# A recurrent two-layer step: one head's turn on TensorE, whole-row transposes through DRAM, and eight matmuls of ones

## The chip, the cores and the metric

The kernel runs on one core of a Trainium2 chip. Its time is the device time of one execution in microseconds. Before the change it takes 2245.49 us, the median of three runs (2245.31 to 2247.33). A core has five engines with one instruction queue each, all served in order: TensorE (PE, with its weight loads as PEld), VectorE (DVE), ScalarE (ACT), GpSimd (POOL) and SyncE (SP), which only issues DMAs here.

## What is computed

One inference step of a two-layer decoder with D = 1024, run for a prompt of 1024 tokens and for 8 samples of one token each, with the same weights. Cut to what matters:

```
for layer in (even, odd):
    shift, scale, gate = split(silu(c) @ ada_w[layer] + ada_b[layer])
    h = rms(x) * (1 + scale) + shift
    even: gated delta rule, 8 heads of 128x128; mLSTM, 8 heads of 64x128
        h_b = sigmoid(o_pre) * rms(mlstm(q_b, k_b, v_b, i, f))
    odd:  gated linear attention (GLA), 4 heads of 128x256; retention, 4 heads of 128x256
    y = concat(branch outputs) * silu(z)        # 2048 wide
    x = x + gate * (y @ w_out)
y = rms(x), and the new states of every head, for prompt and samples
```

All of it is float32, chunk by chunk over the prompt.

## The kernel before

Prompt and samples stand side by side as W = 1032 columns, features on the 128 partitions (feature layout). A matmul of float32 accuracy is three matmuls of values split into a high and a low part (hi x hi, hi x lo, lo x hi) over three pieces of NB = 344 columns. The high part is a rounding copy on ScalarE (`whi`, or an activation tile such as `s_h`), the low part a subtraction on VectorE or POOL (`wlo`). Weights come in blocks of 128 columns (`wf` loaded, `whi`, `wlo`). PSUM banks are named `pj` (three, projections), `A` (three) and `B` (two). SBUF tiles are named slots that are used over and over: `s_zz`, `s_mp`, `s_va` and so on.

Nothing is issued where it is written. A class `Recorder` collects every operation with its operands, and its `order` (line 274) plans the whole program as a list schedule, ten times forward and backward, by a table of costs (`_cost`, line 106, and `_pe_cost`, line 136), and keeps the order with the shortest plan. `emit` (line 443) then issues it, so that every row of the profile has line 448, and rows are told apart by tiles. An edit anywhere can change the order on all engines.

At the start, the ada matmuls of the even layer run group by group (g = 0 to 3), each from four 512-KB loads of `in_ada_w` that lie in free slots. They give the scale and shift of two feature tiles (through bank B, `s_qg` and `base`), and with these VectorE makes h in pieces of 344 columns (`s_aT`, `s_Y` and others in, `s_h` out). The first weight block is projected into the A banks as the h tiles come.

In the even layer each gated-delta head h makes `s_q` (line by line: a causal convolution of four taps in `s_pt`, then SiLU), normalizes it, and multiplies keys with queries (A<-s_q,s_k). The gates of all heads are scanned once; their values go from row layout to token layout through DRAM (`ed` written from `s_Y`, read as `s_N`).

An mLSTM head ends with its output in token layout, `hn`, in slot `mp`. `mlstm_out` (line 1525) turns it to feature layout: `squares` (line 1697) transposes 32x32 squares of a whole 128x1024 tile in one VectorE instruction, writes it to DRAM (`td`) in four DMAs and reads it back in one; four VectorE products with the norm weight and the output gate (`zz`) follow. Heads 0 to 6 write the product to DRAM (`yd`); head 7 keeps it for the output projection, as its 16th block (k = 15).

`out_proj` (line 1943) splits the 16 blocks of y into high and low parts, each in one piece of 1032 columns (`split`), where k = 14 and 15 are used last (`late`). They multiply weights kept in `s_zz` (even) or `s_tmp` (odd).

In the odd layer a GLA or retention head needs its keys in token layout (`kt`, slot `N`). `by_token` (line 1690) makes them by 16 VectorE transposes of 32x256, one for each pair of 32-row squares; values go through `squares` (`v_tokens`, line 1710), followed by a copy on ScalarE. Retention scales its keys on ScalarE after that.

## Time and profile before

| | |
|---|---|
| runs | 2247.33, 2245.31, 2245.49 us |
| profiled execution | 2242.51 us, of which 2240.7 us span |
| mean granted TensorE clock | 0.989 |
| TensorE busy | 2174.0 us (97%), 17532 matmuls |
| VectorE busy | 1307.6 us (58%) |
| ScalarE, POOL busy | 762.3 us (34%), 586.7 us (26%) |
| DMA | 290.62 MB, 130 GB/s on average |

Times are microseconds from the start of the span. A row of the timeline has start, duration, engine, line, operation, output tile, input tiles, shape and count, and in brackets the idle time of the engine ahead of it with what ended that. Busy times of TensorE overlap between neighbours (an instruction's end is modelled), so the distance between starts is what one costs. The layout of time by the loads of weights: those of the even layer's output projection are issued from 1078.8 to 1276.0 us, those of the odd layer's input projection from 1287.3 to 1962.5, and those of its output projection from 1974.4 to 2183.1.

### The profile page before, as it was taken

How to read it: one execution, taken by the hardware profiler on the slowest of the kernel's cores; microseconds unless marked ns; L12 is line 12 of the kernel's file. 1: busy time of each engine (PE TensorE's matmuls, PEld its weight loads, DVE VectorE, ACT ScalarE, POOL GpSimd, SP SyncE). 2: the span in 40 equal slices, each digit the busy share in tenths (PEclk: the TensorE clock that was granted, in tenths of full speed). 3: DMA queues.
4: the chain of work that ended last, by engine and by line, in shares of the span. 5: the costliest groups of instructions: out<-in, count | busy, mean ns of one | idle time of the engine just before them, and what ended most of it. 6: DMA issues, size and time to landing. Idle time of an engine off the chain costs nothing.

```text
span 2240.7 us, 42464 instructions
## 1 busy us (share of the span) xinstructions
PE 2174.0 (97%) x17532; PEld 2027.2 (90%) x17532; DVE 1307.6 (58%) x2559; ACT 762.3 (34%) x1374; POOL 586.7 (26%) x409
## 2 busy tenths in 40 slices
PE   6989999999999999999989999999999999999998
PEld 4877788898999899899989999999999999999997
DVE  6766747575665758576553265745754754756322
ACT  4422323232423333232331134235234334334322
POOL 3121222111221212211330042523523522534110
PEclk9999999999999999998999999999999999999999
DMA  9466564436352544346483223344253253365212
GB/s 265 125 205 149 168 174 145 120 90 175 89 152 66 171 124 121 108 120 155 134 237 109 65 77 85 88 144 124 68 168 111 77 162 117 96 183 197 69 59 93
DMA packets 343352, 290.62 MB, mean 130 GB/s; under 512 B 51963, under 2 KB 315637, under 8 KB 343150
## 3 DMA queue, kind: packets, MB, share of 16 engines
q1 hardware_dynamic: 343158, 287.91, 44.6%
q8 instruction: 137, 2.24, 0.4%
q14 instruction: 57, 0.47, 0.1%
HBM read 213.61 MB, written 74.44 MB: 129 GB/s over the span
## 4 chain that ended last, share of the span: by engine, by line
PE 80%; DVE 8%; DMA 7%; issue 2%; POOL 1%; ACT 1%; SPq 1%; POOLq 0%; DVEq 0%; ACTq 0%
PE pj L448 63%; PE A L448 12%; PE B L448 4%; DMA s_tmp<-sd 1%; SPq L448 1%; DVE arena L448 1%; DVE s_pt L448 1%; DVE s_tmp L448 1%; DMA s_tmp<-in_state_gla 1%; DVE s_N L448 1%; POOL s_qg L448 1%; DVE s_zz L448 1%; DVE wlo L448 1%; DVE s_h L448 1%; DMA s_Y<-rd 1%
## 5 line engine op out<-in xcount | busy, mean ns | idle before, releaser
L448 PE MATMUL pj<-s_h,whi 128*128 128x344 f32 (+1 forms) x6024 | 1487.4, 326 | 3.5 <-ACT whi L448 1.3
L448 PEld LDWEIGHTS pj<-s_h,whi 128*128 128x128 f32 (+1 forms) x6024 | 1038.7, 188 | 33.2 <-issue 20.8
L448 PE MATMUL pj<-s_h,wlo 128*128 128x344 f32 (+1 forms) x3024 | 978.3, 324 | 0.2 <-DVE s_h L448 0.2
L448 PEld LDWEIGHTS pj<-s_h,wlo 128*128 128x128 f32 (+1 forms) x3024 | 568.4, 188 | 11.8 <-issue 8.8
L448 DVE TENSOR_TENSOR wlo<-wf,whi 128x1024 fp32r<-128x1024 f32 x112 | 146.4, 1307 | 220.5 <-ACT whi L448 217.2
L448 ACT ACTIVATE whi<-wf 128x1024 fp32r<-128x1024 f32 (+1 forms) x146 | 152.1, 1042 | 330.6 <-PE pj L448 298.1
L448 ACT ACTIVATE s_pt<-pj 128x344 f32<-128x344 f32 (+1 forms) x170 | 76.9, 453 | 228.4 <-PE pj L448 228.1
L448 POOL TENSOR_TENSOR wlo<-wf,whi 128x1024 fp32r<-128x1024 f32 (+1 forms) x32 | 81.4, 2545 | 170.5 <-ACT whi L448 170.5
L448 POOL TENSOR_TENSOR arena<-arena,base 128x8 f32<-128x8 f32 (+5 forms) x38 | 61.1, 1612 | 241.2 <-DVE arena L448 232.7
L448 POOL TENSOR_TENSOR s_tmp<-s_EM 128x512 f32<-128x512 f32 (+1 forms) x60 | 78.7, 1326 | 106.7 <-DVE s_N L448 28.4
L448 DVE SCALAR_TENSOR_TENSOR s_pt<-s_u,base,s_pt 128x1024 f32<-128x1024 f32 x72 | 100.4, 1395 | 0.3
L448 ACT ACTIVATE s_u<-pj 128x344 f32<-128x344 f32 x93 | 41.6, 453 | 160.1 <-PE pj L448 96.7
L448 DVE SCALAR_TENSOR_TENSOR arena<-arena,A 128x128 f32<-128x128 f32 (+1 forms) x84 | 32.8, 390 | 87.7 <-PE A L448 86.9
L448 DVE SCALAR_TENSOR_TENSOR s_zz<-s_pt,pj 128x344 f32<-128x344 f32 x96 | 48.8, 508 | 52.3 <-ACT s_pt L448 51.9
L448 POOL MEMSET s_u<- 128x3 f32 x24 | 2.5, 104 | 267.6 <-DVE s_pt L448 267.6
L448 ACT ACTIVATE arena<-A,arena 128x128 f32<-128x128 f32 x64 | 23.5, 367 | 119.6 <-PE A L448 119.5
L448 ACT ACTIVATE s_tmp<-s_tmp 128x1024 f32<-128x1024 f32 (+1 forms) x44 | 46.2, 1059 | 48.4 <-POOL s_tmp L448 40.8
L448 POOL TENSOR_TENSOR s_tmp<-s_tmp,arena 128x1024 f32<-128x1024 f32 (+2 forms) x26 | 44.4, 1711 | 69.3 <-PE A L448 43.5
L448 POOL TENSOR_TENSOR s_kd<-s_kd,s_vs 128x1032 f32<-128x1032 f32 x8 | 20.4, 2547 | 159.1 <-ACT s_vs L448 159.1
L448 DVE TENSOR_TENSOR s_EM<-s_EM 64x15 f32<-64x15 f32 (+7 forms) x240 | 51.5, 215 | 17.2 <-DMA s_EM<-nd 12.0
L448 DVE SCALAR_TENSOR_TENSOR arena<-arena,B 64x130 f32<-64x130 f32 (+1 forms) x84 | 31.2, 372 | 51.0 <-PE B L448 49.8
L448 ACT ACT_TABLE_LOAD x41 | 52.6, 1283 | 5.2 <-DMA s_h<-in_x_prompt 4.5
(639 smaller groups left out, 3543.4 us busy)
## 6 DMA issues: line engine op xcount, KB each, us to landing
wf<-in_ev_w_in SPq DMA_DIRECT2D x64, 512.0 KB
wf<-in_od_w_in SPq DMA_DIRECT2D x48, 512.0 KB
wf<-in_ada_w SPq DMA_DIRECT2D x32, 512.0 KB
s_tmp<-sd SPq DMA_DIRECT2D x24, 512.0 KB
s_pt<-yd SPq DMA_DIRECT2D x16, 516.0 KB
td<-s_kd SPq DMA_DIRECT2D x64, 128.0 KB
td<-s_vs SPq DMA_DIRECT2D x64, 128.0 KB
s_v<-td SPq DMA_DIRECT2D x16, 512.0 KB
```

Of the source, the lines that this page charges most:

```text
L448: op.fn(*[self.placed(x) for x in op.args], **{k: self.placed(x) for k, x in op.kw.items()})
```

## The change

Four edits:

- `mlstm_out` of head 7 turns `hn` by eight 128x128 transposes on TensorE, into two B banks of 512 columns, and two VectorE products read these banks. The other seven heads go on as before.
- `by_token` is gone. `tokens` puts the keys of both odd mixers through `squares` (one VectorE transpose of 128x1024, four DMAs out, one back) and a ScalarE copy, which for retention also scales.
- `split` takes k = 14 and 15 in three pieces of 344 columns, and their low part is always on VectorE (k = 15 was on POOL).
- After the first group's ada work, eight matmuls multiply a constant of ones with columns of `qg` into a bank of A. The first matmul of the first projection into that bank starts its sum anew, so that what they leave is overwritten.

```diff
--- before.py
+++ after.py
@@ -1526,12 +1526,21 @@
         self.side = "B"
         nc, V = self.nc, self.nc.vector
         y = oz
-        hn = hn.rearrange("p c d -> p (c d)")
-        z = self.squares(self.slot("va", name="ht"), hn, hn)
-        y4 = y[:, 0:T].rearrange("p (c a j) -> p c a j", c=NC, a=4)
-        for i in range(4):
-            V.scalar_tensor_tensor(y4[:, :, i, :], z[:, :, i, :], self.nw[:, 1:2], y4[:, :, i, :], op0=ALU.mult,
-                                   op1=ALU.mult)
+        if h < 7:
+            hn = hn.rearrange("p c d -> p (c d)")
+            z = self.squares(self.slot("va", name="ht"), hn, hn)
+            y4 = y[:, 0:T].rearrange("p (c a j) -> p c a j", c=NC, a=4)
+            for i in range(4):
+                V.scalar_tensor_tensor(y4[:, :, i, :], z[:, :, i, :], self.nw[:, 1:2], y4[:, :, i, :], op0=ALU.mult,
+                                       op1=ALU.mult)
+        else:
+
+            for g in range(2):
+                t = self.ps()
+                for i in range(4):
+                    self.tr(t[:, 128 * i:128 * i + 128], hn[:, 4 * g + i, :])
+                s = slice(512 * g, 512 * g + 512)
+                V.scalar_tensor_tensor(y[:, s], t, self.nw[:, 1:2], oz[:, s], op0=ALU.mult, op1=ALU.mult)
         V.tensor_copy(self.ozs[:, h % 2, :], oz[:, T:W])
         if h % 2:
             V.scalar_tensor_tensor(self.nms[:, 0, 0], self.nms[:, 1, 0], self.nw[:, 1:2], self.ozs[:, 0], op0=ALU.mult,
@@ -1687,13 +1696,6 @@
         z = [self.proj_silu2(src, 4112 + 256 * h + 128 * i, "zz") for i in range(2)]
         return q, k, v, z
 
-    def by_token(self, out, x):
-
-        x = x[:, 0:T].rearrange("p (c t) -> p c t", t=L)
-        for i in range(0, 128, 32):
-            for j in range(0, 128, 32):
-                self.nc.vector.transpose(out[j:j + 32, :, i:i + 32], x[i:i + 32, :, j:j + 32])
-
     def squares(self, y, x, z):
 
 
@@ -1707,14 +1709,16 @@
         dma(z.rearrange("p (a x) -> p a x", a=4), d.rearrange("a p x -> p a x"))
         return z.rearrange("p (a c j) -> p c a j", a=4, c=NC)
 
+    def tokens(self, tag, x, z, scale=1.0):
+
+        t = self.slot(tag, name="tok")
+        z = self.squares(t, x, z)
+        self.act(t[:, 0:T].rearrange("p (c a j) -> p c a j", c=NC, a=4), z, AF.Copy, scale=scale)
+        return t
+
     def v_tokens(self, v):
-        vt = []
-        for i, tag in enumerate(("kd", "vs")):
-            t = self.slot(tag, name="vt")
-            z = self.squares(t, v[i], v[i])
-            self.act(t[:, 0:T].rearrange("p (c a j) -> p c a j", c=NC, a=4), z, AF.Copy)
-            vt.append(t[:, 0:T].rearrange("p (c d) -> p c d", c=NC))
-        return vt
+        return [self.tokens(tag, v[i], v[i])[:, 0:T].rearrange("p (c d) -> p c d", c=NC)
+                for i, tag in enumerate(("kd", "vs"))]
 
     def chunks256(self, aT, qg, kt, vt, decay, out):
 
@@ -1834,8 +1838,7 @@
         self.act(t, t, AF.Exp, scale=1.0 / 16)
         kw = self.slot("tmp", [128, T], name="kw")
         V.tensor_tensor(kw, k[:, 0:T], t.rearrange("p c t -> p (c t)"), op=ALU.mult)
-        kt = self.slot("N", name="kt")
-        self.by_token(kt[:, 0:T].rearrange("p (c d) -> p c d", d=128), kw)
+        kt = self.tokens("N", kw, kw)
         vt = self.v_tokens(v)
 
         aT = self.slot("aT", [128, NC, L], name="aT")
@@ -1919,9 +1922,7 @@
     def ret_mix(self, h, q, k, v, z):
         self.side = "B"
         nc, a, V, G = self.nc, self.a, self.nc.vector, self.nc.gpsimd
-        kt = self.slot("N", name="kt")
-        self.by_token(kt[:, 0:T].rearrange("p (c d) -> p c d", d=128), k)
-        self.act(kt[:, 0:T], kt[:, 0:T], AF.Copy, scale=self.rend[:, h:h + 1])
+        kt = self.tokens("N", k, self.slot("EM", name="kz"), scale=self.rend[:, h:h + 1])
         vt = self.v_tokens(v)
         qg = self.slot("qg", name="qg")
         G.tensor_tensor(qg[:, 0:T].rearrange("p (c t) -> p c t", t=L), q[:, 0:T].rearrange("p (c t) -> p c t", t=L),
@@ -1974,8 +1975,10 @@
                 nc.sync.dma_start(t, self.yd[k])
             hi, lo = (self.big[x if isinstance(x, tuple) else (x, 0)][:, 0:W].bitcast(F32R)
                       for x in at[2 * k:2 * k + 2])
-            self.act(hi, t, AF.Copy)
-            (G if k % 3 == 0 else V).tensor_tensor(lo, t, hi, op=ALU.subtract)
+
+            for c in (slice(NB * j, NB * j + NB) for j in range(3)) if k in late else (slice(0, W),):
+                self.act(hi[:, c], t[:, c], AF.Copy)
+                (G if k % 3 == 0 and k not in late else V).tensor_tensor(lo[:, c], t[:, c], hi[:, c], op=ALU.subtract)
             yy.append((hi, lo))
 
         def weights(n, g, ks=8):
@@ -2168,6 +2171,10 @@
             if g == 0:
                 self.load_gates()
                 parts.append((self.load_w(self.a["ev_w_in"][0], 1024), ps[1]))
+            if g == 0:
+
+                for i in range(8):
+                    self.mm(ps[1][0], self.ones, self.big["qg", 0][:, 0:NB])
             self.layer_h0(xr, g)
             for j in range(3):
                 self.stacked(ps[0][j], self.gate_w, j, (2 * g, 2 * g + 1))
```

The order of the instructions is planned anew, and most rows of all engines move. Three places of it follow (numbers behind a slot are those of its buffers and uses).

VectorE, where the first gated-delta head's `s_q` and the gate values `s_N` (read back from `ed`) come, before:

```order
L448 COPY arena<-B_116 128x4x32
L448 SCALAR_TENSOR_TENSOR s_pt_83<-arena,base,s_pt_83 128x8
L448 TENSOR_SCALAR arena<-arena 128x64
L448 TENSOR_TENSOR arena<-s_mq_73,arena 64x8
L448 SCALAR_TENSOR_TENSOR s_pt_83<-arena,base,s_pt_83 128x8
L448 TENSOR_SCALAR arena<-arena 128x64
L448 TENSOR_TENSOR arena<-s_N_70,arena 128x64
L448 TENSOR_TENSOR arena<-arena,s_N_70 128x64
L448 TENSOR_TENSOR s_N_70<-s_N_70 128x64
L448 COPY arena<-s_N_70 128x320
L448 COPY arena<-s_N_70 64x64 x2
L448 SCALAR_TENSOR_TENSOR s_q_64<-s_pt_84,s_pt_83 128x1032
```

And now:

```order
L448 STREAM_TRANSPOSE s_vs_67<-s_v_65 128x1024
L448 SCALAR_TENSOR_TENSOR s_q_64<-s_pt_84,s_pt_83 128x1032
L448 COPY arena<-B_116 128x4x32
L448 COPY arena<-s_q_64 128x2x4
L448 TENSOR_TENSOR arena<-s_k_63,s_q_64 128x8
L448 TENSOR_SCALAR arena<-arena 128x64 x2
L448 TENSOR_TENSOR s_qg_68<-s_q_64,s_qg_68 128x1024
L448 TENSOR_TENSOR wlo_109<-wf_105,whi_107 128x1024
L448 TENSOR_TENSOR arena<-s_N_70,arena 128x64
L448 TENSOR_TENSOR arena<-arena,s_N_70 128x64
L448 TENSOR_TENSOR s_N_70<-s_N_70 128x64
L448 COPY arena<-s_N_70 128x320
```

`s_q` stood behind the operations that read `s_N`; now it stands ahead of them, with six rows between.

TensorE, where the output projection of the even layer begins with blocks in the A and pj banks (`s_mp_78` is head 7's `hn`), now:

```order
L448 MATMUL pj_110<-s_h_713,whi_106 128x344
L448 MATMUL pj_111<-s_h_635,whi_106 128x344
L448 MATMUL pj_111<-s_h_619,wlo_108 128x344
L448 MATMUL pj_111<-s_h_713,whi_106 128x344
L448 MATMUL B_117<-base,s_mp_78 128x128 x4
L448 MATMUL B_116<-base,s_mp_78 128x128 x4
L448 MATMUL A_114<-s_N_9680,wlo_109 128x344
L448 MATMUL A_114<-s_v_10084,whi_107 128x344
L448 MATMUL A_114<-s_k_10098,whi_107 128x344
L448 MATMUL A_114<-s_v_10084,wlo_109 128x344
```

These transposes are new; before, rows of the A and pj banks followed each other there. Later in the same projection TensorE comes to the late blocks k = 14 (`s_va`, `s_kwe`) and k = 15 (`s_qs`, `s_mp`), now:

```order
L448 MATMUL A_113<-s_mq_10264,wlo_108 128x344
L448 MATMUL pj_112<-s_va_10489,s_zz_10405 128x344
L448 MATMUL pj_112<-s_kwe_10495,s_zz_10405 128x344
L448 MATMUL pj_112<-s_va_10489,s_zz_10405 128x344
L448 MATMUL pj_112<-s_qs_10380,s_zz_10405 128x344
L448 MATMUL pj_112<-s_mp_10408,s_zz_10405 128x344
L448 MATMUL pj_112<-s_qs_10380,s_zz_10405 128x344
L448 MATMUL pj_110<-s_va_10489,s_zz_10405 128x344
```

The late blocks come in the same order as before. 144 matmuls of 344 columns lie between the transposes and the first of them.

TensorE, where the output projection of the odd layer comes to its late blocks (k = 14 is the pair of `s_tmp`, k = 15 `s_kd` and `s_vs`, and the weights are `s_tmp_18144`), before:

```order
L448 MATMUL A_113<-s_u_18147,whi_106 128x344
L448 MATMUL A_113<-s_mp_18138,wlo_108 128x344
L448 MATMUL pj_112<-s_tmp_18360,s_tmp_18144 128x344
L448 MATMUL pj_110<-s_tmp_18360,s_tmp_18144 128x344
L448 MATMUL pj_111<-s_tmp_18360,s_tmp_18144 128x344
L448 MATMUL A_114<-s_tmp_18360,s_tmp_18144 128x344
L448 MATMUL A_115<-s_tmp_18360,s_tmp_18144 128x344
L448 MATMUL A_113<-s_tmp_18360,s_tmp_18144 128x344
L448 MATMUL pj_112<-s_tmp_18368,s_tmp_18144 128x344
L448 MATMUL pj_112<-s_tmp_18360,s_tmp_18144 128x344
L448 MATMUL pj_110<-s_tmp_18368,s_tmp_18144 128x344
```

And now:

```order
L448 MATMUL A_113<-s_u_18073,whi_106 128x344
L448 MATMUL A_113<-s_mp_18059,wlo_108 128x344
L448 MATMUL pj_112<-s_tmp_18204,s_tmp_18144 128x344
L448 MATMUL pj_112<-s_tmp_18210,s_tmp_18144 128x344
L448 MATMUL pj_112<-s_tmp_18204,s_tmp_18144 128x344
L448 MATMUL pj_112<-s_kd_18242,s_tmp_18144 128x344
L448 MATMUL pj_112<-s_vs_18251,s_tmp_18144 128x344
L448 MATMUL pj_112<-s_kd_18242,s_tmp_18144 128x344
L448 MATMUL pj_110<-s_tmp_18204,s_tmp_18144 128x344
```

Before, the six banks took the high part of k = 14 first, and k = 15 was mixed in behind; now each bank takes both blocks in turn. From the sums of the last norm (B_116<-s_kd,base 32x258) 180 rows lie between it and this place, where there were 76 before. The eight matmuls of ones are not at the place where TensorE waited for h, but further ahead, around the first transposes of `s_qg`: seven directly behind them, the eighth after one more group of ada matmuls.

## The prediction

> **What bounds the kernel now.** I read the page's first and fourth parts, then the table of stretches, then TensorE's waits in order of size, and last the timeline around each wait that the change touches. The fences show rows of these views; a timeline's row has start, length and, in brackets, the idle time ahead of it with its releaser.
>
> ```profile
> PE 2174.0 (97%) x17532; PEld 2027.2 (90%) x17532; DVE 1307.6 (58%) x2559; ACT 762.3 (34%) x1374; POOL 586.7 (26%) x409
> PE 80%; DVE 8%; DMA 7%; issue 2%; POOL 1%; ACT 1%; SPq 1%; POOLq 0%; DVEq 0%; ACTq 0%
> core 0: us, PE busy (x) PEld busy (x) DVE busy (x) ACT busy (x) POOL busy (x), PEclk, DMA share, GB/s
> 42.00:46.00 4.00, 2.79 (x21) 1.96 (x21) 4.00 (x9) 2.31 (x6) 2.76 (x3) 0.50 0.91 252
> 46.00:50.00 4.00, 4.00 (x23) 3.52 (x16) 3.04 (x11) 2.92 (x10) 1.64 (x3) 0.57 1.18 290
> 138.00:142.00 4.00, 3.06 (x14) 3.06 (x15) 3.96 (x5) 0.69 (x4) 3.48 (x2) 0.53 0.85 268
> 142.00:146.00 4.00, 4.00 (x16) 2.11 (x15) 1.24 (x6) 1.87 (x2) 0.00 (x0) 0.62 0.61 147
> 1176.00:1180.00 4.00, 3.59 (x14) 3.59 (x15) 2.54 (x3) 0.77 (x2) 0.35 (x1) 0.59 0.62 171
> 1300.00:2000.00 700.00, 697.13 (x6201) 664.89 (x6200) 417.23 (x626) 275.22 (x434) 276.31 (x171) 1.00 0.39 114
> ```
>
> TensorE is busy 2174.0 of 2240.7 us, so only 66.7 us of it is idle, and a gain has to come from these or from stretches at half clock. The column before the last two is the granted clock: it falls to about a half after some gaps, so a gap costs more than its own length. In the second layer, from 1300 to 2000 us, TensorE lacks 2.87 us of 700 at clock 1.00. There, relief of any other engine is worth next to nothing. TensorE's waits that the change can reach stand below, each with its row: 4.27 and 3.77 us near the start, 2.92 and 2.07 at the end of the first layer, 1.16 and 1.49 at the end of the second, 15.7 us in all.
>
> Any edit lets the planner order all five engines anew, so I price each place by the new order and the old durations.
>
> **The start: eight matmuls of ones.** No row has them; the nearest is three f32 matmuls of a constant over 344 columns.
>
> ```profile
> 25.59 1.97 PE L448 MATMUL A<-s_N,base 128*128 128x344 f32 x6 [0.76 <-DVE s_N L448]
> 42.93 0.66 PE L448 MATMUL A<-s_h,whi 128*128 128x344 f32 x1 [4.27 <-ACT s_h L448]
> 62.01 0.66 PE L448 MATMUL B<-base,s_qg 128*128 128x128 f32 x4 [1.00 <-ACT s_qg L448]
> 28.09 1.23 DVE L448 TENSOR_TENSOR s_aT<-s_tmp,s_q 128x1032 f32<-128x1032 f32 x1 [1.53 <-ACT s_q L448]
> 32.58 0.29 DVE L448 TENSOR_REDUCE s_qg<-B 128x36 f32<-128x144 f32 x1
> 70.84 0.16 DVE L448 TENSOR_TENSOR s_h<-base,s_h 128x8 fp32r<-128x8 f32 x1
> 50.00:60.00 10.00, 10.00 (x22) 1.00 0.35 96
> ```
>
> Three took 1.97 us in six records, so eight cost 8 x 0.66 = 5.3 us. The planner does not put them at 42.93 - 4.27 = 38.7, where TensorE waits for the first h, but right behind the first transposes of s_qg, which in the old trace are the row at 29.06 (quoted below) and end at 29.7. They push the small ada matmuls back by at most 5.3 us, about what the gap behind those can take, and they run ahead of the gap, not in it. So I expect the gap before the first h, and a half clock behind it, to stay.
>
> Suppose they did hold the clock. The clock reads 0.50 at 42 to 46 and 0.57 at 46 to 50, so it is half until 46 + 0.43 / 0.50 x 4 = 49.4. From 42.93 to 49.4 TensorE would need 3.2 us less. But it then waits for VectorE, which makes h until 70.84 and is busy 10.00 us of the ten from 50 to 60 (the last row, of VectorE alone), 4.00 from 42 to 46 and 3.04 from 46 to 50: at 62.01 TensorE already waits 1.00 us for an s_qg value. The 3.2 us would be waited there.
>
> The Trainium skill, "TensorE: Matmul & The Clock Gate", section "Part 1: The HAM clock gate", says that the rate is half by default and after an idle window of 3.4 us, and full after a busy one, and that the windows run freely. By that rule ones just ahead of h would save the 3.2 us in some executions and not in others, and ones at 29.7 would save nothing. The trace agrees that a gap of 4.27 us costs the clock.
>
> Against it stands VectorE's own order. Now the reduction (was at 32.58) and the wlo subtraction behind it come ahead of the multiply that started at 28.09. The reduction needs TensorE's transposes of 29.06 and so cannot start before 29.7; the multiply that opened the chain loses 29.7 - 28.09 = 1.6 us. Bounds -3.2 and +1.6; since the last h hangs on VectorE, I take +1.0.
>
> **The gate values at 130 to 146 us.**
>
> ```profile
> 129.04 0.18 DVE L448 TENSOR_SCALAR arena<-arena 128x64 f32<-128x64 f32 x1
> 136.26 0.50 DVE L448 TENSOR_TENSOR arena<-s_N,arena 128x64 f32<-128x64 f32 x1 [7.04 <-DMA s_N<-ed]
> 137.65 1.23 DVE L448 SCALAR_TENSOR_TENSOR s_q<-s_pt,s_pt 128x1032 f32<-128x1032 f32 x1
> 138.94 0.79 PE L448 MATMUL A<-s_q,s_k 128*128 128x128 f32 x2 [3.77 <-DVE s_q L448]
> ```
>
> VectorE stood 7.04 us for the gates' way through DRAM, and s_q, which doesn't need them, stood behind it. TensorE waited 3.77 us and then ran at half clock: from 138.94 to 142 + 0.38 / 0.50 x 4 = 145.0, which is 6.1 us of which 3.05 are lost. In the new order s_q stands ahead of the gate rows, directly behind the transpose of s_v. Its last input in the old trace was made by 129.0, so it is ready near 130.5, ahead of 138.94 - 3.77 = 135.2, where TensorE ran dry. That removes 3.77 + 3.05 = 6.8 us. What waits next is the mask product (s_aT<-A,s_EM), which needs the gates at 136.3; TensorE has projection matmuls between. Bounds: -6.8, and 0 if the stop only moves to that product; I take -6.3.
>
> **The end of the first layer.**
>
> ```profile
> 1147.19 1.92 POOL L448 TENSOR_TENSOR s_mp<-s_mp,arena 128x1024 f32<-128x1024 f32 x1
> 1146.28 0.32 PE L448 MATMUL A<-s_N,wlo 128*128 128x344 f32 x1
> 1159.30 2.06 SPq L448 DMA_DIRECT2D td<-s_va  x4
> 1171.10 1.67 DVE L448 SCALAR_TENSOR_TENSOR s_zz<-s_mp,base,s_zz 128x256 f32<-128x256 f32 x4
> 1170.36 0.32 PE L448 MATMUL pj<-s_va,s_zz 128*128 128x344 f32 x1
> 1170.52 0.32 PE L448 MATMUL pj<-s_kwe,s_zz 128*128 128x344 f32 x1
> 1173.91 0.42 PE L448 MATMUL pj<-s_qs,s_zz 128*128 128x344 f32 x1 [2.92 <-ACT s_qs L448]
> 1176.41 0.66 PE L448 MATMUL pj<-s_mp,s_zz 128*128 128x344 f32 x1 [2.07 <-POOL s_mp L448]
> 29.06 0.66 PE L448 MATMUL B<-base,s_qg 128*128 128x128 f32 x4 [0.71 <-ACT s_qg L448]
> ```
>
> The last mLSTM head was normalized by 1149.11, but its way to feature layout through DRAM was only issued at 1159.30, its products came at 1171.10, and behind them came ScalarE's copy and POOL's subtraction. TensorE waited 2.92 + 2.07 = 4.99 us, then at half clock until 1176 + 0.82 x 4 = 1179.3 by the 0.59 of that stretch, 2.9 us with 1.4 lost. Together 6.4 us.
>
> Now eight transposes (two rows like that of 29.06) cost TensorE 2 x 0.66 = 1.3 us. In the new order 144 matmuls of 344 columns lie between them and the first that needs the result, 23 us at the 0.16 us by which the starts at 1170.36 and 1170.52 lie apart. Two products, three copies and three VectorE subtractions fit in that, even with some wlo work between. The DMA round trip of five issues is gone as well. But the transposes wait for hn on TensorE itself: the matmul that follows them in the new order began at 1146.28 in the old, with nine others now put ahead (9 x 0.16 = 1.4 us), so TensorE is there near 1147.7 less what the earlier parts gain for both; hn came at 1149.11, so 0 to 1.4 us, or 2.8 without the nine; the new VectorE order moves the tail of that chain forward, so I take 1.0. Term: -6.4 + 1.3 + 1.0 = -4.1 (bounds -6.4 + 1.3 = -5.1 and -6.4 + 1.3 + 2.8 = -2.3).
>
> **The end of the second layer.** The split of k = 14 and 15 in three pieces and the freed VectorE bear here.
>
> ```profile
> 2060.48 2.82 POOL L448 TENSOR_TENSOR wlo<-wf,whi 128x768 fp32r<-128x768 f32 x1
> 2061.97 0.64 PE L448 MATMUL B<-s_kd,base 128*32 128x258 f32 x8
> 2071.03 2.41 POOL L448 TENSOR_TENSOR s_qg<-s_qg,s_aT 128x1032 f32<-128x1032 f32 x1 [7.74 <-DMA s_aT<-rd]
> 2076.96 0.74 PE L448 MATMUL pj<-s_tmp,s_tmp 128*128 128x344 f32 x3 [1.16 <-DVE s_tmp L448]
> 2081.55 0.42 PE L448 MATMUL pj<-s_vs,s_tmp 128*128 128x344 f32 x1 [1.49 <-POOL s_vs L448]
> ```
>
> The last norm runs from the sums at 2061.97 over DRAM to POOL's two multiplies and a subtraction. TensorE waited 1.16 + 1.49. In the new order 180 matmuls, 28 us, lie between the sums and the first matmul of k = 14, against the 15 us that the old trace had, and the last subtraction is on VectorE in pieces. Both waits should go: -2.6. POOL now has a 768-column wlo (2.8 us) behind the first multiply; TensorE wants it 126 matmuls or 20 us after the sums, and it would be done 2071.03 + 2.41 + 2.8 = 2076.2, 14.3 us after. It is covered by 5 us; without cover it would cost what is missing. Bounds -2.6 and +2.
>
> **The second layer's middle.**
>
> ```profile
> L448 DVE STREAM_TRANSPOSE s_N<-s_qs 32x256 f32<-32x256 f32 x64 | 27.9, 436 | 5.1 <-DMA yd<-s_N 4.2
> L448 DVE STREAM_TRANSPOSE s_N<-s_tmp 32x256 f32<-32x256 f32 x64 | 27.7, 433 | 1.0
> L448 DVE STREAM_TRANSPOSE s_kd<-s_u 128x1024 f32<-128x1024 f32 x8 | 9.9, 1236 | 12.9 <-ACT s_u L448 12.7
> L448 ACT ACTIVATE s_kd<-s_u 128x1024 f32<-128x1024 f32 x8 | 8.4, 1055 | 5.9 <-DMA wf<-in_od_w_in 5.3 <-DMA s_u<-td 0.6
> 1548.41 1.78 SPq L448 DMA_DIRECT2D td<-s_kd  x4
> 1552.15 0.38 SPq L448 DMA_DIRECT2D s_u<-td  x1
> ```
>
> VectorE loses 27.9 + 27.7 = 55.6 us and gains eight transposes of 1.24, net -45.7; ScalarE gains four copies of 1.06 (retention had one already), 4.2 us; SyncE gains 8 x 5 DMAs. VectorE's work lies beside TensorE, which lacks 2.87 us in all of this stretch: at most -2.9, taken as 0. Elsewhere (200 to 1150 us) the new order moves waits about with no cause that I can name: 0, with 5 us either way.
>
> **Sum:** +1.0 - 6.3 - 4.1 - 2.6 = -12.0 on the profiled execution, whose span of 2240.7 us lies in a time of 2242.5, 1.8 more. The profiled one is 3.0 below the median of the runs, 2245.5; I set the difference against the median: 2233.5 us.
>
> **Rivals.** (1) *The gains are given back.* TensorE arrives earlier at waits for values that have their own chains: the gates at 136.3, or the first h. For it: one chain goes over DRAM, the other over a VectorE that hardly rests. Against it: TensorE has projection matmuls ahead in every such place. If the gates' stop only moves (0 for -6.3) and the start loses 1.6, the sum is +1.6 - 4.1 - 2.6 = -5.1; with hn waited for 2.1 instead of 1.0 it is -4.0, 2241.5 us.
>
> (2) *Slower: SyncE's queue in the second layer.* The read back from td waits for its four writes, and everything behind it in the queue, weight loads too, stands. In the rows above the four issues end at 1550.19 and the read goes at 1552.15, so 1.78 + 1.96 + 0.38 = 4.1 us of queue for each of eight new round trips, 33 us. If TensorE had no lead and waited all of it, the sum is -12 + 33 = +21, 2266 us. It decides from 12.0 / 8 = 1.5 us per trip. Against it: sixteen such trips (v, two halves of eight heads) are there now and TensorE lacks only 2.87 us.
>
> (3) *The ones hold the clock and h is not VectorE's.* -3.2 for +1.0: 2245.5 - 16.2 = 2229.3. That is the change doing what its words say; the new order speaks against it. The opposite, that the ones do nothing, is part of my forecast.
>
> **How the numbers follow.** Forecast 0.50, between 2226 and 2239; rival 1, 0.26, of which 0.15 within 4.5 us of the old median and 0.11 below that; rival 2, 0.12; rival 3, 0.12. About 0.2%, 4.5 us, is what a measurement of this kernel can tell from no change. Faster 0.50 + 0.12 + 0.11 = 0.73, same 0.15, slower 0.12. The range goes from 2223 (rival 3 with the 5 us of the unnamed stretches) to 2245, which takes in rival 1 and leaves out rival 2 and some below.
>
> **What would show it.** Right: no wait of TensorE for s_q above 1 us and clock 1.00 in the stretch that answers to 138 to 146; none for the two late operands of either output projection; a wait of up to 2 us in front of transposes B<-base,s_mp; the half clock at 43 to 49 still there, or gone with a longer wait near 62. Wrong: TensorE idle grown between 1300 and 2000 for whi or DMA wf (rival 2), a new wait of several us for s_aT or arena near 140 (rival 1), or a last h earlier than 69 (rival 3).

## The result and the profile after

The changed kernel takes 2230.89 us, the median of five runs (2224.66 to 2235.22), against 2245.49 us of the kernel before (2243.39 to 2247.33) beside it: 0.9933 of its time, 95% interval 0.9917 to 0.9950. That is faster by 14.6 us, where 12.0 had been forecast. The profiled execution is the slowest of the five, with 2235.22 us and a span of 2233.4. A second profile, taken later, has 2225.1, and both are used below.

The page's row of busy times, then the table of stretches, after the change (columns as in the prediction: busy time and instructions of PE, PEld, DVE, ACT and POOL, then granted clock, DMA share, GB/s):

```profile
PE 2174.2 (97%) x17556; PEld 2030.1 (91%) x17556; DVE 1268.2 (57%) x2446; ACT 764.7 (34%) x1386; POOL 572.4 (26%) x407
40.00:45.00 5.00, 1.58 (x4) 1.22 (x5) 5.00 (x10) 2.40 (x7) 1.83 (x2) 0.61 0.75 203
45.00:50.00 5.00, 5.00 (x29) 4.35 (x31) 5.00 (x13) 2.96 (x10) 3.14 (x5) 0.71 1.19 299
135.00:140.00 5.00, 5.00 (x18) 4.39 (x17) 3.00 (x5) 3.08 (x7) 1.45 (x1) 0.50 0.99 348
1170.00:1180.00 10.00, 10.00 (x65) 10.00 (x65) 4.14 (x11) 1.34 (x3) 0.00 (x0) 1.00 0.64 208
1300.00:2000.00 700.00, 694.53 (x6168) 661.99 (x6167) 379.52 (x509) 279.59 (x439) 272.53 (x169) 1.00 0.43 125
```

VectorE is lighter by 39.4 us, which is nothing in itself. The half clock at the first h (43 to 49 us) is still there. So is one at 135 to 140, where the prediction had none. At 1170 to 1180 it is gone. Between 1300 and 2000 TensorE now lacks 5.47 us, against 2.87 before.

The timeline's rows of TensorE after, at the places that the prediction spoke of:

```profile
43.14 0.66 PE L448 MATMUL A<-s_h,whi 128*128 128x344 f32 x1 [3.23 <-ACT s_h L448]
110.74 0.58 PE L448 MATMUL pj<-s_h,whi 128*128 128x344 f32 x2 [0.97 <-ACT s_u L448]
133.76 1.92 PE L448 MATMUL pj<-wf,base 128*32 128x512 f32 x4 [2.47 <-DMA wf<-in_ada_w]
1141.04 1.09 PE L448 MATMUL B<-base,s_mp 128*128 128x128 f32 x8
1165.24 0.32 PE L448 MATMUL pj<-s_qs,s_zz 128*128 128x344 f32 x1
1165.40 0.32 PE L448 MATMUL pj<-s_mp,s_zz 128*128 128x344 f32 x1
1495.92 0.77 PE L448 MATMUL B<-s_qg,arena 128*128 128x128 f32 x2 [2.80 <-DVE arena L448]
2017.28 0.49 PE L448 MATMUL B<-s_kd,s_N 128*128 128x128 f32 x2 [1.41 <-ACT s_N L448]
2070.65 0.63 PE L448 MATMUL pj<-s_tmp,s_tmp 128*128 128x344 f32 x3
2071.28 0.32 PE L448 MATMUL pj<-s_vs,s_tmp 128*128 128x344 f32 x1
```

The waits for s_q, for s_qs and s_mp at the end of the first layer, and for s_tmp and s_vs at the end of the second have all gone (rows without brackets did not wait). Three large ones are new: for a block of ada weights at 133.76, for VectorE at 1495.92, for ScalarE's s_N at 2017.28. So are two smaller ones: 0.97 us for ScalarE's s_u at 110.74, and 1.38 us at 1404.88 (A<-s_q,s_k), for which the profile shows no releaser.

Where the time went is read by the same operation in two profiles: how much later or earlier it starts. The table gives what each interval between two such operations gained (minus) or lost, in us. The last measured column is the mean of seven profiles (two of the changed kernel, five of its close variants), less the mean of three (two of the kernel before, one of its variant with s_q moved); the runs are below.

| interval (times of before) | this profile | second profile | means, 7 less 3 | predicted |
|---|---|---|---|---|
| to A<-s_N,base, 25.6 | -1.0 | 0.0 | +0.2 | 0 |
| the start, to 114.4 | +1.2 | +1.2 | +1.2 | +1.0 |
| the gates, to 187.3 | -1.0 | -3.9 | -2.4 | -6.3 |
| 187.3 to 964.2 | -1.3 | -1.8 | -1.4 | 0 |
| 964.2 to 1170.4, transposes included | -3.5 | -6.7 | -3.3 | +2.3 |
| late blocks, 1170.4 to 1305.6 | -6.8 | -6.8 | -6.7 | -6.4 |
| second layer, 1305.6 to 2074.6 | +8.4 | +5.7 | +5.9 | 0 |
| 2074.6 to 2231.3 | -3.2 | -3.3 | -3.3 | -2.6 |
| sum | -7.2 | -15.6 | -9.8 | -12.0 |

The +2.3 is the transposes' 1.3 and the wait of 1.0 for hn.

An interval is only comparable where it holds the same work. TensorE, from the operation at 114.4 to the one at 187.3, before and after:

```profile
114.44:187.26 72.82, 66.46 (x396) 0.95 0.70 205
```

```profile
114.61:186.45 71.84, 68.25 (x414) 0.95 0.75 203
```

The new order puts 18 more matmuls into it, ten of the projection (344 columns) and eight of 130 columns, which before stood behind 187.3. By the distances of such starts (0.16 and some 0.12 us) that is about 2.5 us of work, an estimate. With it set apart the gates gained 3.5, 6.4 and 4.9 us (the three measured columns), and 187.3 to 964.2 gained nothing: it lost 1.1 in the means. In the second layer and behind it the counts are the same before and after.

### The profile page after: what moved, and what is told of

Same layout as the page of the kernel before. It is cut to its first block, busy times and chain, and to the rows that moved or that the text cites. A ratio compares the mean times of both kernels' runs of the same rounds, so it can differ in the third digit from the quotient of the medians.

```text
span 2233.4 us, 42459 instructions
## 1 busy us (share of the span) xinstructions
PE 2174.2 (97%) x17556; PEld 2030.1 (91%) x17556; DVE 1268.2 (57%) x2446; ACT 764.7 (34%) x1386; POOL 572.4 (26%) x407
## 5 line engine op out<-in xcount | busy, mean ns | idle before, releaser
L448 PEld LDWEIGHTS pj<-s_h,wlo 128*128 128x128 f32 (+1 forms) x3024 | 569.0, 188 | 11.1 <-issue 9.1
L448 ACT ACTIVATE s_tmp<-s_tmp 128x1024 f32<-128x1024 f32 (+1 forms) x44 | 46.2, 1058 | 39.4 <-POOL s_tmp L448 31.5
```

Source lines behind the costliest of these rows:

```text
L448: op.fn(*[self.placed(x) for x in op.args], **{k: self.placed(x) for k, x in op.kw.items()})
```

## The experiments

All ratios are to the kernel before on the same chip (medians 2241.67, 2242.29 and 2242.82 us for the three groups of four). "Span" is the profiled execution's.

| kernel | median us | ratio, 95% | span us |
|---|---|---|---|
| change again | 2228.21 | 0.9937 (0.9921 to 0.9954) | 2225.1 |
| before again | 2241.60 | 0.9998 (0.9986 to 1.0009) | 2231.9 |
| change without ones | 2231.17 | 0.9959 (0.9944 to 0.9974) | 2229.3 |
| ones just ahead of h | 2227.57 | 0.9936 (0.9923 to 0.9949) | 2217.5 |
| before, s_q moved ahead | 2239.14 | 0.9988 (0.9975 to 1.0000) | 2241.3 |
| change, ada block later | 2226.84 | 0.9932 (0.9919 to 0.9945) | 2225.2 |
| change, copy earlier | 2226.69 | 0.9932 (0.9916 to 0.9949) | 2232.2 |
| change, both | 2228.18 | 0.9930 (0.9915 to 0.9944) | 2235.0 |
| head 7's turn alone | 2233.38 | 0.9959 (0.9946 to 0.9973) | 2239.1 |
| the split alone | 2234.27 | 0.9957 (0.9941 to 0.9973) | 2233.4 |
| tokens alone | 2244.20 | 1.0006 (0.9988 to 1.0024) | 2242.5 |
| the ones alone | 2234.22 | 0.9960 (0.9942 to 0.9979) | 2231.9 |

### The same two kernels again: how far does one profile carry?

The edit is none: the change, and the kernel before, as they are.

> The changed kernel once more, unchanged. In its first five runs it took 2224.7 to 2235.2 us, with a mean granted clock of 0.995 to 0.991. Theory A (the spread is the TensorE clock): in each run the span less what the clock lost, (1 - clock) x span, comes to the same 2211 to 2214 us, and a second profile has the half clock at some of the same waits but not at all of them. Theory B (the spread is in the waits, DMAs above all): that difference scatters by as much as the spans do, some 10 us, and the waits of the two profiles differ by several us.

> The kernel before once more, unchanged. Its five runs took 2243.4 to 2247.3 us, the one known clock is 0.989. Theory A: span less clock loss is 2216 +- 1.5 us in every run, which is 3 to 5 us above that of the changed kernel, so that of the 14.6 us between the medians only some 4 to 5 us are waits and work and the rest is clock lost behind the waits. Theory B: the clock is about the same in both kernels on average and the 14.6 us are waits.

The second profile of the change is 8.3 us shorter than the first, that of the kernel before 8.8 us. What differs is the granted clock. The first five runs of the change have spans of 2233.4, 2228.9, 2231.2, 2222.9 and 2229.1 us at mean clocks of 0.991, 0.993, 0.991, 0.995 and 0.992; span times clock is 2213.3, 2213.3, 2211.1, 2211.8 and 2211.3. So a span splits into what is left at full clock and what the clock takes, (1 - clock) x span. The clock is on record to 0.001, which is 2.2 us of a span. What the clock takes scatters from 11 to 25 us over eleven runs of the change. (It holds idle time at a low clock too, as at the start and the end.) What is left scatters less, but more than theory A allowed: from 2207.6 to 2214.3 over these eleven, and from 2209.4 to 2220.6 over 46 runs of the kernel before (the twelve of this one, and 17 each beside the first two groups). On average the two parts are 2215.1 and 24.8 us over these 46, and 2211.2 and 16.2 over the eleven. Of some 12.5 us between the mean spans, 3.9 are thus work and waiting, and 8.6 are clock: theory A holds for the averages.

The rows show where the clock differs, TensorE alone, clock in the third column from the end, first the kernel before in its first profile:

```profile
1055.00:1060.00 5.00, 5.00 (x51) 0.50 0.01 2
```

The kernel before in its second profile, with its wait for s_q:

```profile
137.09 0.49 PE L448 MATMUL A<-s_q,s_k 128*128 128x128 f32 x2 [3.57 <-DVE s_q L448]
135.00:140.00 5.00, 2.91 (x20) 1.00 0.90 297
1055.00:1060.00 5.00, 5.00 (x46) 1.00 0.01 3
```

The same order of instructions ran at half clock at 1055 to 1060 in one execution and at full clock in the other, with TensorE busy in both. And a gap of 3.57 us cost nothing behind it, where the 3.77 us of the first profile had cost 3.05. The prediction had counted those 3.05 as a saving in every execution.

### The ones, left out, and put where the gap is

Without the eight ones, the order of all else kept (what they compute is overwritten anyway):

```diff
-        for i in self.order():
+        seq = self.order()
+        seq = [i for i in seq if not 246 <= i <= 253]
+        for i in seq:
```

> The changed kernel's own order on every engine, with the eight matmuls of ones left out when it is issued; nothing else moves. Prediction's theory (h hangs on VectorE, and the ones stand far ahead of the gap): no difference, within 1.5 us of the changed kernel, and the first projection still at 43 us at half clock. Rival (the ones hold the clock): 2 to 3.2 us slower.

And twelve matmuls of ones by ones over 128 columns into the same bank, directly ahead of the first matmul of h, in their place:

```diff
+        seq = [i for i in seq if not 246 <= i <= 253]
+        ones = self.ops[246]
+        for i in seq:
             op = self.ops[i]
+            if i == 292:
+                w = ones.kw["lhsT"]
+                p = self.placed(ones.args[0])
+                for _ in range(12):
+                    ones.fn(bass.AP(p.tensor, p.offset, [p.ap[0], [1, 128]]), lhsT=w, rhs=w, start=True, stop=True)
```

> The changed kernel's own order, with the eight matmuls of ones left out and twelve of 128 columns, ones times ones, about 3 us in all, issued directly ahead of the first matmul of h, where TensorE waits 3.2 us. Rival 3 of the prediction: the clock is full where it was half, from 43 to 49 us, and the end is 3 us earlier. Prediction's theory: the clock may be full there, but the 3 us are waited for h at about 61 us, and the end moves by less than 1 us.

In the changed kernel most of the ones are this row (two records for each matmul). The last of them ends at 33.3, and the gap only begins at 43.14 - 3.23 = 39.9:

```profile
27.75 4.21 PE L448 MATMUL A<-s_qg,base 128*128 128x344 f32 x14
```

With the ones moved into the gap (TensorE's rows, then its stretches):

```profile
40.53 2.94 PE L455 MATMUL A<-base 128*128 128x128 f32 x24
44.20 0.42 PE L456 MATMUL A<-s_h,whi 128*128 128x344 f32 x1 [0.72 <-ACT s_h L456]
62.04 0.66 PE L456 MATMUL B<-base,s_qg 128*128 128x128 f32 x4 [1.53 <-ACT s_qg L456]
40.00:45.00 5.00, 3.90 (x41) 1.00 0.70 186
45.00:50.00 5.00, 4.24 (x25) 1.00 1.18 303
```

The clock holds at 1.00 from 40 to 50, and that does not help: the wait at 62 is 1.53 us, where the kernel before had 1.00 and the change 0.85, and from 25.6 to 114.4 the interval loses 1.0 us, against 1.2 with the ones early and 1.2 with none at all. From the operation at 25.6 to pj<-base,s_u at 99.8 it takes 74.1 to 74.2 us in all three, and 74.2 in the kernel before. The start hangs on VectorE's h, as predicted; the loss comes behind it, in the wait for s_u at 110.74 (0.97, 1.01 and 0.72 us with the ones early, none and late; none before).

The ones are not without effect, though. Over the runs of these two kernels and of the change beside them, the share of the span that the clock takes differs:

| kernel | runs | clock's part of the span, us: lowest, median, highest |
|---|---|---|
| change, first and second time | 11 | 11.1, 15.6, 24.6 |
| ones just ahead of h | 5 | 11.1, 15.6, 24.5 |
| change without ones | 6 | 20.1, 22.3, 26.9 |

Where it goes is far from the start. TensorE's stretch of the change without ones, then that of the second profile of the change:

```profile
1055.00:1060.00 5.00, 5.00 (x31) 0.50 0.02 3
```

```profile
1055.00:1060.00 5.00, 4.99 (x39) 1.00 0.34 106
```

Summed over 5-us stretches from 1040 to 1100, the clock takes 6.8 us in the profile without ones, 0 in this one, 1.7 in the change's first. It is no rule: the kernel with both moves (below), which has the ones, loses 8.5 us there. Through what eight matmuls at 28 to 33 us bear on the clock a millisecond later, no run shows. About 1.7 us of the difference is only the start itself, where idle time at half clock (5.1 us of loss in most profiles without ones, 3.4 with) gives way to ones at full clock, without an earlier h. What is left of the span at full clock is 3.4 us shorter without the ones (2207.8 against 2211.2 on average), so only a part of the 6.7 us reaches the time: in the median, leaving the ones out costs 3.0 us (2231.17 against 2228.21), and the two intervals overlap. That is the rival's size, but not at its place.

### The gates: s_q moved ahead in the kernel before

The kernel before with its order kept, and one VectorE row, the first head's s_q, moved ahead of the rows that read s_N:

```diff
+MOVES = [([1017], 705)]
...
-        for i in self.order():
+        seq = self.order()
+        for ids, at in MOVES:
+            seq = [i for i in seq if i not in ids]
+            n = seq.index(at)
+            seq[n:n] = ids
+        for i in seq:
```

> The kernel before with one row moved: VectorE's s_q, which stood behind the rows that read the gates, is issued ahead of them; every other row keeps its place. Prediction's step for the gates: TensorE's wait of 3.6 to 3.8 us for s_q goes, and with it the half clock of up to 3.05 us that followed in one of two profiles, so that from the first A<-s_q,s_k on everything is 4 to 7 us earlier. Rival (the stop moves): TensorE runs on into its next stop, the ada matmuls of the next layer (pj<-wf,base) whose load came at about 139 to 142 us, and waits there for wf<-in_ada_w; less than 1.5 us are won.

VectorE's s_q and TensorE's wait in this kernel:

```profile
130.28 1.23 DVE L460 SCALAR_TENSOR_TENSOR s_q<-s_pt,s_pt 128x1032 f32<-128x1032 f32 x1 [1.09 <-ACT s_pt L460]
139.37 1.05 PE L460 MATMUL pj<-wf,base 128*32 128x512 f32 x4 [2.60 <-DMA wf<-in_ada_w]
```

s_q is made at 130.28, near the 130.5 that the prediction worked out, and no matmul waits for it. But TensorE stops at the next thing: a block of ada weights that has not landed. The interval from 114.4 to 187.3 is 0.2 us shorter than in the first profile of the kernel before and 0.6 longer than in its second; the median is 0.12% lower, and the 95% interval ends at 1.0000. So the stop moved; it didn't go, as the rival said.

### The ada block moved, the copy moved, and both

In the changed kernel, the matmuls of that ada block go behind thirteen projection matmuls and nine of A<-s_q,s_k and A<-s_k, by the same loop as above:

```diff
+MOVES = [([1495, 1496, 1497, 1498, 1499, 1500, 1501, 1502, 1503, 1504, 1505, 1506, 1507, 1053, 1054, 1055, 1060, 1061, 1062, 1067, 1068, 1069], 1545)]
```

> The changed kernel's order with 22 rows of TensorE moved: 13 projection matmuls and the nine A<-s_q,s_k and A<-s_k, which stood behind the ada matmuls pj<-wf,base, are issued ahead of them, some 4 us of work. Theory (the load of ada weights took the place of the wait for s_q): the wait of 1.6 to 2.5 us at 134 us goes and nothing takes its place, so that behind 150 us everything is 1.6 to 2.5 us earlier, up to 5.5 where the half clock had followed. Rival (the gates at 136 are the real limit): the wait reappears as one for s_EM or arena within 20 us.

In the second layer, VectorE's copy arena<-B goes ahead of three products of s_tmp that wait for a DMA:

```diff
+MOVES = [([13053, 13054, 13055], 13056)]
```

> The changed kernel's order with one row moved: at 1489 to 1496 us VectorE's copy of bank B into arena, which stood behind three products that wait for the state rows (DMA s_tmp<-sd), is issued ahead of them. Theory (what was lost in the second layer is VectorE's queue behind a late DMA, not the ScalarE copies or the new round trips themselves): TensorE's wait of 1.9 to 2.8 us there goes, with the 1.7 to 3.4 us of half clock behind it, and the end is 2 to 6 us earlier. Rival (SyncE's queue is late as such): the wait turns into another of the same head, and the end moves by less than 1 us.

And both moves in one kernel:

> The changed kernel's order with both moves, that of ada_late and that of copy_early. If both theories hold, the gains add: 3.5 to 5 us less waiting than the changed kernel, whose runs had medians of 2228 and 2231 us, so 2222 to 2227 us, less where the clock is kept. If either rival holds, it is within 2 us of the better of the two.

First the changed kernel's own rows: VectorE's s_q, then SyncE's issues, then how busy the DMA engines were from 124 to 134 us in 40 slices (tenths) and what they moved.

```profile
126.95 1.19 DVE L448 SCALAR_TENSOR_TENSOR s_q<-s_pt,s_pt 128x1032 f32<-128x1032 f32 x1
120.73 2.68 SPq L448 DMA_DIRECT2D ed<-s_Y  x3
124.64 0.36 SPq L448 DMA_DIRECT2D wf<-in_ada_w  x1
DMA  0000009979000189998997909061441325999999
GB/s 33 0 0 0 0 0 115 49 33 33 0 0 0 82 262 197 147 66 33 66 66 33 49 0 66 33 47 37 39 55 57 61 94 209 332 311 301 305 297 305
```

The 512-KB load is issued at 124.64 and TensorE goes on at 133.76, 9.1 us later. For most of that time the DMA engines move at most 66 GB/s, where 300 and more follow. The writes of the gates to `ed` had been issued just ahead; that they are what slows the load was not tried by itself. Then the kernel with the ada block later:

```profile
141.84 1.77 PE L460 MATMUL pj<-wf,base 128*32 128x512 f32 x4 [2.33 <-DMA wf<-in_ada_w]
137.29 1.27 SPq L460 DMA_DIRECT2D wf<-in_ada_w  x2
```

The wait at 133.76 is gone, and one of 2.33 us stands at 141.84, in front of the next ada block: its load is issued only at 137.29. The theory that nothing would take the wait's place has fallen. What ends last in both orders is a block of ada weights.

The copy's move did what was expected in its place. VectorE in the changed kernel, then with the copy moved:

```profile
1494.16 1.27 DVE L448 SCALAR_TENSOR_TENSOR s_tmp<-s_tmp,s_qs,s_tmp 128x256 f32<-128x256 f32 x3 [5.92 <-DMA s_tmp<-sd]
1495.36 0.42 DVE L448 COPY arena<-B 128x256 f32<-128x256 f32 x1
```

```profile
1493.71 0.42 DVE L460 COPY arena<-B 128x256 f32<-128x256 f32 x1 [4.63 <-PE B L460]
```

TensorE's wait of 2.80 us and the half clock behind it (0.52 and 0.80 in the stretches from 1495 and 1500, about 3.0 us lost) are not in this kernel, and the second layer up to 1646.8 loses 0.3 us instead of 5.5 (3.1 in the second profile of the change). Behind that it loses more than the change, 6.1 us against 2.9 and 2.6, with half clock near 2015 and 2035. And in three other profiles without the move (no ones, ones just ahead of h, ada later) this wait was 0.67 us or less: the copy stands behind a DMA, and only in some executions does that DMA end last. Both moves together, with 2228.18 us, are within 2 us of the better of the two, as the rivals said. The three ratios, 0.9930 to 0.9932, are not apart from one another, nor from the change's 0.9937. So none of these kernels is shown to be faster than the change.

### Each part of the change alone

Each with the diff of the change for that part, in the kernel before, with a plan of its own. Head 7's eight transposes:

```diff
+        if h < 7:
...
+        else:
...
+                for i in range(4):
+                    self.tr(t[:, 128 * i:128 * i + 128], hn[:, 4 * g + i, :])
```

> The kernel before with the first edit alone (head 7 turned by TensorE), planned anew. Prediction's step for the end of the first layer: the way through DRAM is what was late, so this edit alone removes both waits at the late blocks (2.9 + 2.1 us) and the half clock behind them, for 1.1 us of transposes; from the first late matmul to the first of the A banks it takes 2.8 us as in the changed kernel instead of 9.1 to 9.6; in the end 4 to 7 us faster than before. Rival (the low part on POOL in one piece was late too): the wait for POOL s_mp stays, 2 us or more.

The split of the two late blocks:

```diff
-            (G if k % 3 == 0 else V).tensor_tensor(lo, t, hi, op=ALU.subtract)
...
+                (G if k % 3 == 0 and k not in late else V).tensor_tensor(lo[:, c], t[:, c], hi[:, c], op=ALU.subtract)
```

> The kernel before with the third edit alone (k = 14 and 15 in three pieces, low part on VectorE), planned anew. At the end of the first layer the head's way through DRAM stays late: the wait for ScalarE stays and only that for POOL s_mp goes (2 us of 5). At the end of the second layer, prediction's step: the waits of 1.2 and 1.5 us go or shrink below 0.5. Rival (it was VectorE's relief or the new order, not the pieces): both stay. Overall 2 to 5 us faster, which is at the limit of what the runs can tell.

Head 7's turn alone (TensorE's rows):

```profile
1152.28 1.09 PE L448 MATMUL B<-base,s_mp 128*128 128x128 f32 x8
2074.76 0.74 PE L448 MATMUL pj<-s_tmp,s_tmp 128*128 128x344 f32 x3 [1.14 <-DVE s_tmp L448]
2079.33 0.43 PE L448 MATMUL pj<-s_vs,s_tmp 128*128 128x344 f32 x1 [1.47 <-POOL s_vs L448]
```

It takes 6.8 us from the late blocks of the first layer and leaves the waits of the second, as expected of it; in time it gains 9.4 us, more than the 4 to 7 expected. The load in SyncE's queue ahead of the way through DRAM, in the kernel before:

```profile
1158.84 0.37 SPq L448 DMA_DIRECT2D wf<-in_ev_w_out  x1
```

The split alone (SyncE, VectorE, ScalarE, VectorE, TensorE at the first layer's end; the last row is the second's):

```profile
1155.05 0.38 SPq L448 DMA_DIRECT2D wf<-in_ev_w_out  x1
1155.48 2.47 SPq L448 DMA_DIRECT2D td<-s_va  x4
1168.52 1.67 DVE L448 SCALAR_TENSOR_TENSOR s_zz<-s_mp,base,s_zz 128x256 f32<-128x256 f32 x4
1170.22 1.25 ACT L448 ACTIVATE s_qs<-s_zz 128x344 fp32r<-128x344 f32 x3 [2.88 <-DVE s_zz L448]
1170.74 1.37 DVE L448 TENSOR_TENSOR s_mp<-s_zz,s_qs 128x344 fp32r<-128x344 f32 x3 [0.56 <-ACT s_qs L448]
1171.18 0.31 PE L448 MATMUL pj<-s_qs,s_zz 128*128 128x344 f32 x1
2071.57 0.59 PE L448 MATMUL pj<-s_tmp,s_tmp 128*128 128x344 f32 x2 [1.41 <-DVE s_tmp L448]
```

This was not expected: with head 7 still going through DRAM, the same interval loses 6.7 us of its length, all of what the transposes removed. Two things did it. The way through DRAM starts 3.8 us earlier (its four writes at 1155.48, before at 1159.30; in both they go out right behind a load of wf, issued at 1158.84 and here at 1155.05). And the operands come in pieces: the first matmul of s_qs starts at 1171.18, 0.96 us after ScalarE began with the first piece, instead of behind a copy of 1032 columns and POOL's subtraction. How much is due to the earlier start, which is the new order's, and how much to the pieces, was not tried apart. So each of the two edits, with its own order, removes the whole of the same wait, and together they remove it once. In time the split alone gains 8.6 us, more than the 2 to 5 expected. At the end of the second layer the expectation failed as well: the wait for s_vs is gone, but TensorE still waits 0.69 us (at 2068.97) and 1.41 us for s_tmp.

The keys by whole-tile transposes and DRAM:

```diff
-        kt = self.slot("N", name="kt")
-        self.by_token(kt[:, 0:T].rearrange("p (c d) -> p c d", d=128), kw)
+        kt = self.tokens("N", kw, kw)
...
+        kt = self.tokens("N", k, self.slot("EM", name="kz"), scale=self.rend[:, h:h + 1])
```

> The kernel before with the second edit alone (keys of the second layer through DRAM), planned anew. Prediction: TensorE lacks 1 to 3 us of the second layer either way, so no difference, within 3 us of before. Rival (its round trips make TensorE wait): the second layer has 2 to 6 us more of idle time and half clock, for ScalarE's copy s_N among others, and the kernel is no faster or slower than before. What the plan does elsewhere adds 3 us either way.

VectorE's groups of the two transposes in the changed kernel (busy time, then mean ns of one), and TensorE's new wait in the kernel with the tokens alone:

```profile
L448 DVE STREAM_TRANSPOSE s_N<-s_qs 128x1024 f32<-128x1024 f32 x4 | 5.0, 1244 | 4.1 <-DMA yd<-s_N 4.1
L448 DVE STREAM_TRANSPOSE s_N<-s_tmp 128x1024 f32<-128x1024 f32 x4 | 4.8, 1212 | 0.1
```

```profile
2025.04 0.49 PE L448 MATMUL B<-s_kd,s_N 128*128 128x128 f32 x2 [1.74 <-ACT s_N L448]
```

VectorE's 55.6 us have become 9.8, a saving of 45.8. The time stays: 1.0006. In the last retention head the keys come 1.3 to 2.1 us late in every kernel with this edit, since four writes, a read and a scaled copy on ScalarE stand where VectorE worked alone. The interval 1305.6 to 2074.6 loses 3.8 us, and the last one gains 3.2, since here the waits for s_tmp and s_vs are gone, without the split: it is this edit, with VectorE's relief and the new order, that removes both.

The eight ones alone:

```diff
+            if g == 0:
+
+                for i in range(8):
+                    self.mm(ps[1][0], self.ones, self.big["qg", 0][:, 0:NB])
```

> The kernel before with the fourth edit alone (eight matmuls of ones), planned anew. Prediction: they are far ahead of the gap and h hangs on VectorE, so no difference, within 3 us; the markers at 60 to 115 us move by less than 1.5 us. Rival (they keep the clock): 3 us faster with the first projection at full clock.

With 2234.22 us this kernel is 8.6 us faster than the one before, and its profile has none of it at the start: 0.7 us are lost between 25.6 and 114.4. The gain is spread from 114 to 1170, and what the clock takes is 17.9 us in the median of twelve runs (11.1 to 29.1), against 24.6 (17.9 to 31.5) in 28 runs of the kernel before beside it. Neither "no difference" nor the rival's place came. This is the same sign and size as above, where the ones were left out of an order that was kept. It holds through all twelve kernels timed: the medians of the clock's part lie between 13.4 and 17.9 us for the six with ones, and between 22.3 and 25.8 for the six without. So the ones do take some 5 to 7 us off the clock's part, not at the place where they stand. The edit alone also has a plan of its own: it is the only one of the four that puts s_q ahead of the gates (TensorE waits 2.02 us for wf<-in_ada_w at 133.89, where the other three wait 3.7 to 5.3 us for s_q). So part of the 8.6 us is order, and how the ones reach the clock stays open.

The parts alone give -9.4, -8.6, +1.4 and -8.6 us, -25.2 in all, nearly twice what the whole gives. The first two remove the same wait, and each part comes with a plan of its own.

## Why the prediction came out right, and which of its steps did not

**The start** was right in that the gap and the half clock stay and that h hangs on VectorE. That its +1.0 lies near the measured +1.2 is luck. The step was that VectorE's multiply, 1.6 us late, makes h late; but counted from the operation at 25.6 the last h comes 0.1 us later than before (at 69.95, before at 70.84), and up to 99.8 nothing is lost. The +1.2 that was measured is 0.97 us of waiting for s_u at 110.74, which the prediction did not have. Rival 3 fell as it was put, since even ones that do hold the clock there (ones just ahead of h) give nothing before 114.4. But "the ones do nothing", which the prediction called part of its forecast, fell too: the clock takes 5 to 7 us less with them, elsewhere. No term of the sum stood for that.

**The gates** failed in the mechanism. The step was "That removes 3.77 + 3.05 = 6.8 us". Its first half held: s_q is made at 126.95, and nothing waits for it. But the prediction looked for what waits next at the mask product and asked only whether TensorE has matmuls in between. It had, and among them are those of an ada block whose weights land at 133.7. Rival 1 named the kind of thing, a stop that moves, at the wrong operand. The second half, 3.05 us of half clock, wasn't a fixed price: the kernel before itself ran this place at clock 1.00 in another execution. What was gained there came in part from elsewhere: in the first profiles the stop shrank by 1.3 us (2.47 for 3.77), while two waits ahead of it, of 1.06 us for VectorE's s_mp at 117.40 and 1.31 for ScalarE's whi at 127.27, went altogether. Measured: -1.0 and -3.9 in two profiles, -2.4 on average, or some -4.9 with the work set apart that the new order puts there.

**The end of the first layer** was right in what goes, and too small: -6.7 for -6.4 at the late blocks. The 1.3 us of transposes measured 1.1 (1.09 in the row, some of it beside neighbours). The wait of up to 2.8 us for hn did not come at all, in any profile. And "its way to feature layout through DRAM" wasn't the only thing late there: the split alone, with that way kept, removes as much, though its order also starts that way 3.8 us earlier.

**The end of the second layer.** Both waits went, -3.3 for -2.6. Of the two causes that the prediction named, the split in pieces alone leaves 2.1 us of waiting for s_tmp, and the edit that frees VectorE removes both waits alone. Ahead of them stand the new waits that the prediction did not have. **The second layer's middle**, taken as 0, lost 5.9 us. That is rival 2's place and direction, at a sixth of its price, and mostly by another mechanism: TensorE does not wait for weight loads there, but for the keys themselves (1.41 us at 2017.28), at 1404.88 (1.38 us, cause open), and for a copy that VectorE holds behind a DMA (2.80 us and some 3.0 of half clock at 1495.92, in some executions). SyncE's queue may have a part in the last: the read `s_tmp<-sd` stands in it behind a weight load that waited 2.6 us for POOL's wlo, against 1.2 in the kernel without ones; what it would be without that, no run shows. At -45.7 us of VectorE the step named the cover correctly and did not ask what the longer way of the keys would be late for.

**The rest**, 0 with 5 us either way, gained 1.4 up to 964 and, with the transposes' 1.1 set apart, 4.4 more up to 1170: 5.8 in all. With the 2.5 us of work that moved from here to the gates set apart it is 3.3, within the 5 us. The largest piece is clock at 1040 to 1100: 6.8 us lost in the first profile of the kernel before, 1.7 in its second, and 0 or 1.7 in six of seven profiles with ones (8.5 in the seventh).

So the sum was near because parts of it compensated: the gates gave about 1.4 us less than forecast and the second layer with its tail 2.6 + 2.6 = 5.2 less, while the late blocks with the transposes and hn gave 1.5 more and the stretches without a named cause about 3.3 more. That the total came so near is luck. By medians the gain (14.6 and 13.5 us in two comparisons) is larger than the 9.8 of the profiles' means, since one of the two profiles of the kernel before was the shortest of its twelve runs. Some 8.6 us of the gain between the mean spans are clock, where the sum had 3.05 + 1.4. (Rival 3 with 5 us off is 2224.3 by the prediction's own numbers, not the 2223 at which its range begins.)

## What to carry to other kernels

When a wait is to be removed, ask of the engine's next instructions, one by one, whether their own operands are there, weight loads too: here the stop at 138.94 only moved to a load, and then to the next load. Two edits that relieve the same late operand are worth one of them, so price them as alternatives (6.8 and 6.7 us alone, 6.7 together). When a profile is cut into intervals, count the instructions in each: here 2.5 us of work changed its interval and looked like a loss in one and a gain in the next. Where TensorE is 97% busy, look at a second profile before a stretch at half clock goes into a sum as if it were fixed.

## What the runs showed of the hardware

The clock was the largest difference between executions of one kernel: it took 11 to 25 us of some 2230 in eleven runs of the change. And eight matmuls, 5 us of work at the start, went with 5 to 7 us less of it, most of that in the rest of the program, though in the one order that was run with and without them the medians are only 3.0 us apart. What it takes in a place comes in steps: 1.7, 3.4 or 3.5, 5.1 or 5.2, 6.8 or 6.9, once 8.5 us, in nearly every stretch of the profiles that lost any.

A gap and the half clock behind it did not go together by length. Waits of 3.77 us (first profile of before, 3.05 us lost) and 2.47 us (the change, 0.50 from 135 to 140) cost the clock, and 3.57 us (second profile of before) did not. The second profile of the change, behind a wait of 1.88 us and then behind one of 1.59 us:

```profile
1489.11 0.46 PE L448 MATMUL B<-s_qg,arena 128*128 128x128 f32 x2 [1.88 <-DVE arena L448]
1490.00:1495.00 5.00, 5.00 (x29) 0.67 0.62 199
134.01 1.05 PE L448 MATMUL pj<-wf,base 128*32 128x512 f32 x4 [1.59 <-DMA wf<-in_ada_w]
135.00:140.00 5.00, 5.00 (x39) 1.00 1.03 361
```

The shorter one cost nothing, the longer one a third of the clock over 5 us. The Trainium skill, "TensorE: Matmul & The Clock Gate", section "Part 1: The HAM clock gate", says that the windows run freely, so that it depends on where in a window work falls. That gaps of 3.57 and 3.77 us had two prices agrees with it. The Trainium skill, in the same section, also puts the return to half rate at one idle window, about 3.4 us; here gaps of 1.88 and 2.47 us went with it, with TensorE busy for 1.53 and 1.46 us of the 3.4 us up to the fall, and the measurement decides.
